# A transformer block with product-key experts on one core: picks turned into one PSUM bank, smaller one-hots, and another order at five places

## The chip, the core and the metric

The program runs on one core of a Trainium2 chip. Each time is the device time of one execution, in microseconds. The engines of a core are TensorE (PE, its weight loads PEld), VectorE (DVE), ScalarE (ACT), GpSimd (POOL) and SyncE (SP); each executes its own instructions in order and waits on semaphores for the others. PE's clock has two levels, 1.2 and 2.4 GHz; a granted clock of 1.00 in the profile is the higher, 0.50 the lower.

## What is computed

512 tokens of 1024 numbers (float32) pass through one block, cut here to what matters:

```python
h = rms_norm(x, norm1_g)
u_a, v_a, q, k, v = split(h @ w_in)          # 5 x 512 columns
a_out = spatial_gating(gelu(u_a), gelu(v_a), ...)
b_out = dilated_attention(rope(q), rope(k), v)
x = x + concat(rms_norm(a_out), rms_norm(b_out)) @ w_out
# experts: 128 x 128 keys, 8 heads, 16 picks a head
xb = rms_norm(x, norm2_g)
s = einsum('thpc,pkc->thpk', (xb @ w_query).reshape(T, 8, 2, 128), sub_keys)
s1, i1 = top_k(s[:, :, 0], 16); s2, i2 = top_k(s[:, :, 1], 16)
sc, ci = top_k((s1[..., :, None] + s2[..., None, :]).reshape(T, 8, 256), 16)
e = i1[ci // 16] * 128 + i2[ci % 16]
act = gelu(einsum('td,thkd->thk', xb, expert_u[e]))
x = x + einsum('thk,thkd->td', softmax(sc) * act, expert_v[e])
out = rms_norm(x, final_norm_g)
```

## The kernel before

float32 products are made of three: each operand is split into a high part (a cast, "hi") and a remainder (a subtraction, "lo"), and PE adds hi x hi, lo x hi and hi x lo. The stages follow one another:

- **A, to about 241 us.** `proj` (L231) makes five groups of 512 columns, each in four PSUM banks `acc`, or three and a bank of `pu`. Around its matmuls stand the eviction of q with the norm's factor (`qraw`, L270), which needs the sums of squares of all tokens (`xsq`, L309: four passes on ACT) and a root; the rotation of q and k; and the gelu of v (`va`, L373). `warm(f)` is an ACTIVATE on one element that makes ACT load the function table of f ahead of its first use; ACT holds one table at a time. Attention and the output projection follow.
- **B, to about 344 us.** `query(c)` and `scores(c)` give the key scores, `top16` sorts them on DVE.
- **C, to about 404 us.** `decode` (L648) turns the place of each pick among the candidates into its two keys. For each pick it writes row and column number 16 times beside each other (casts on ACT, L681), compares with 0..15 (L688), multiplies by the sorted list of keys (L690) and adds up in four halvings (L695, L697): 16 x 16 elements a pick and key. The dense token blocks are decoded in three calls, of 9, 9 and 6 heads times blocks; the last block's two calls of 4 lie in stage E. Meanwhile `ahead(n, limit)` issues n matmuls of the next U blocks (scores of all 384 dense tokens against 128 experts, 24 matmuls of 128 x 384 a block). For a block `part` casts uhi on ACT, ulo is made on GpSimd (`part_lo`) or later on DVE (`los`), and `flush` applies the gelu (`act`, L768). `turn(b)` (L818) then transposes the picks of 128 tokens on PE: two key numbers (idxT) and the gate gT, each through a bank of its own.
- **D, about 404 to 541 us.** The dense weights of 384 tokens and all 16384 experts, in 48 steps of 8 tokens. `hots(t8)` (L847) makes one-hots of the second key (`ohb`, 16 rows of 128) and of the first key times the gate (`oha`: 8 tokens, each with the gate's high and low part, 16 rows), both on DVE, two steps ahead. PE multiplies them in 16 matmuls (L896) into two banks, `put` evicts them on ACT (L876) to `wst`, and every fourth step is stored to DRAM in four DMAs on ACT's queue (`store`, L884). Between the steps PE makes some ten U matmuls.
- **E and F, about 546 to 1474 us.** 128 experts' rows: `vproduct` adds 18 matmuls of 128 x 512 for each to six banks `acc` (three token blocks x two halves); in E 24 U matmuls stand beside them. The last token block has its experts' rows gathered by index instead, and worked through on DVE.
- **G.** The final sum, norm and store: `final_sum`, `gain`, `root`, `finish` for each token block.

What sets the order is the code itself: the engines' instructions are issued in the order in which the loops are written, `ahead` filling in. Tiles of a pool rotate over `bufs` buffers, and an instruction that writes one waits for the readers of its last use.

Of the kernel before, what the change touches and what calls it, by code (L numbers as in the profile page):

```python
# [20 lines left out]
NB = 4  # L21
# [19 lines left out]
UVB = 4  # L41
SLOW = 0.35
# [3 lines left out]
def peer_block(ctx: ExitStack, tc: tile.TileContext, A, out):  # L46
# [182 lines left out]
    warm(AF.Copy)  # L229
# [142 lines left out]
    for b in range(NB):  # L372
        S.activation(va[:, b, :], ps[b], AF.Gelu_apprx_tanh, scale=xrs[:, b:b + 1], accum_out=lns[:, 0, b:b + 1])  # L373
# [274 lines left out]
    def decode(pool, lists, ci, outs):  # L648
# [3 lines left out]
        tl = lambda nm, dt: pool.tile(PK, dt, name=nm)  # L652

# [35 lines left out]
        for p, o in enumerate(o4):
            V.tensor_tensor(o, o, fi.rearrange("p h b s k -> p (h b) s k")[:, :, p, None, :].to_broadcast(wide),  # L690
                            op=ALU.mult)
        yield
        for w in (8, 4, 2):
            for o in o4:
                V.tensor_tensor(o[:, :, :, 0:w], o[:, :, :, 0:w], o[:, :, :, w:2 * w], op=ALU.add)  # L695
        for oh, o in zip(ohs, outs):
            V.tensor_tensor(o, oh[:, :, :, :, 0], oh[:, :, :, :, 1], op=ALU.add)  # L697
# [15 lines left out]
    HG = (3, 3, 2)  # L713
    route = [rt.tile([128, DB, H, TOPK], F32, name=f"route{i}") for i in range(3)]
# [38 lines left out]
    def pick_head(h):  # L753
# [3 lines left out]
        for n in HG:  # L757
            if h == h0 + n - 1:
                steps.append(decode(rt, dense[1][:, h0:h0 + n], ci[:, h0:h0 + n], [r[:, h0:h0 + n] for r in by_head]))
            h0 += n  # L760
# [57 lines left out]
    def turn(b):  # L818

        rows = []  # L820
        for nm, t, dt, scale in (("i2T", route[1], BF16, 1.0), ("i1T", route[0], BF16, 1.0),
                                 ("gT", route[2], F32, GSCALE)):
            ps = pr.tile([128, 512], F32, name="po" if nm == "i2T" else "tr")
            T.transpose(ps[:, :128], t[:, b].rearrange("p h k -> p (h k)"), ident)
            if nm == "i2T":

                idx = rt.tile([128, 16, 2, 8, 2], BF16, name="idxT", bufs=2)
            r = idx[:, :, len(rows), :, :] if dt is BF16 else rt.tile([128, 16, 8, 2], F32, name=nm)
            S.activation(r, ps[:, :128].rearrange("p (g t) -> p g t", t=8)[:, :, :, None].to_broadcast([128, 16, 8, 2]),
                         AF.Copy, scale=scale)  # L830
# [16 lines left out]
    def hots(t8):  # L847
# [3 lines left out]
        idx, gw = tsc[b]  # L851
# [6 lines left out]
        wide = [128, 2, 8, NK // 2, 2]  # L858
        V.tensor_tensor(a.rearrange("p (s t) (k two) -> p s t k two", s=2, two=2),  # L859
                        c[:, None, 8:16].rearrange("p o t (k two) -> p o t k two", two=2).to_broadcast(wide),  # L860
                        gw[:, g, :, :, None, :].to_broadcast(wide), op=ALU.mult)
        return a, c

# [3 lines left out]
    hot = [hots(0), hots(1)]  # L867
    ahead(24, AHEAD)
# [17 lines left out]
    for t8 in range(N8):  # L886
# [43 lines left out]
    h2 = gp.tile([128, 1024], F32, name="h2")  # L930

    def gather_routing():
# [13 lines left out]
        def decoded(h):  # L946
            return decode(gp, late[1][:, h:h + 4], gci[:, h:h + 4], [r[:, h:h + 4] for r in groute])
# [66 lines left out]
    def vsplit(e):  # L1014
        if e in vraws:
            hi = ex.tile([128, 1024], F32R, name="vhi")
            lo = ex.tile([128, 1024], F32R, name="vlo")
# [10 lines left out]

    def wsplit(e):
        if e in wmuls:  # L1030
            hi = ex.tile([128, DT], F32R, name="wahi")
            lo = ex.tile([128, DT], F32R, name="walo")
# [11 lines left out]
    for _ in range(3):  # L1044
# [66 lines left out]
    for e in range(NK):  # L1111
# [8 lines left out]
        if routing is not None:  # L1120
# [20 lines left out]
        if e == NK - 3:  # L1141
# [7 lines left out]
        if e == NK - 8:  # L1149
# [91 lines left out]
```

## Time and profile before

| | |
|---|---|
| median of 3 executions | 1488.34 us (1487.87 to 1490.42) |
| the profiled execution | 1490.96 us, span 1489.2 |
| granted clock, mean | 0.996 |
| PE busy | 1453.4 us |
| DVE busy | 1159.6 us |
| ACT busy | 641.3 us |
| GpSimd busy | 283.6 us |

The span goes from the first instruction to the last. A busy share is an average over all stages, so what an edit in one of them is worth is read from that stretch of the trace, not from this table. PE is the engine with the most work throughout; the question at each place is what it waits for there.

### The profile page before, as it was taken

Reading aid. Unit: us, or ns where it says so; the run is one execution under the profiler, and the core shown is the slowest. Engines: PE = TensorE matmul, PEld = TensorE weight load, DVE = VectorE, ACT = ScalarE, POOL = GpSimd, SP = SyncE. Lnnn points to the kernel's source line nnn. Section 1 sums busy time; section 2 is a strip of 40 time slices with the busy share of each in tenths; the row PEclk is TensorE's granted clock in tenths of the full one; section 3 lists DMA queues with packets and bytes.
Section 4 is the critical chain, followed back from the end, with each engine's and each line's share of the span. In section 5 each row is a group of like instructions: output and inputs, shape, how many; then the busy total and the mean of one; then the engine's idle time right before and its main releaser. Section 6 shows DMA issues by size and latency. Waiting matters only on the chain.

```text
span 1489.2 us, 21574 instructions
## 1 busy us (share of the span) xinstructions
PE 1453.4 (98%) x7945; PEld 1292.6 (87%) x7945; DVE 1159.6 (78%) x2415; ACT 641.3 (43%) x1088; POOL 283.6 (19%) x222
## 2 busy tenths in 40 slices
PE   8999999999899999999999999999999999999997
PEld 6878988888888899999999999999999999987785
DVE  4745554999899967779878787888787888877775
ACT  5455753344555544434333333333333333323334
POOL 0040002445500000012222222222222222211002
PEclk9999999999999999999999999999999999999999
DMA  6331032232366776469999999999999998988764
GB/s 217 106 99 57 22 114 104 86 91 96 110 230 256 261 291 214 135 228 378 355 351 329 315 338 321 327 334 336 347 326 333 331 328 308 348 286 299 250 212 160
DMA packets 128777, 358.52 MB, mean 241 GB/s; under 512 B 9120, under 2 KB 59808, under 8 KB 112288
## 3 DMA queue, kind: packets, MB, share of 16 engines
q1 hardware_dynamic: 103184, 197.75, 40.1%
q0 software_dynamic: 18432, 134.23, 23.6%
q10 hardware_dynamic: 7056, 25.18, 4.2%
q8 instruction: 62, 1.02, 0.3%
q14 instruction: 43, 0.35, 0.1%
HBM read 327.10 MB, written 30.02 MB: 240 GB/s over the span
## 4 chain that ended last, share of the span: by engine, by line
PE 78%; DVE 9%; DMA 5%; issue 3%; ACT 3%; POOL 1%; ACTq 0%; SPq 0%; DVEq 0%; POOLq 0%
PE pu L201 34%; PE acc L1041 30%; PE acc L252 6%; DMA vraw<-in_uv_dram 3%; DVE ohb L855 3%; DVE oha L859 2%; DVE ulo L181 1%; DMA uraw<-in_uT_dram 1%; PE tr L734 1%; PE pu L252 1%; PE tr L434 1%; POOL ulo L181 1%; PE acc L447 1%; DVE vlo L81 1%; DMA xt<-in_x_dram 1%
## 5 line engine op out<-in xcount | busy, mean ns | idle before, releaser
L201 PE MATMUL pu<-h2T,uhi 128*128 128x384 f32 (+2 forms) x2336 | 451.0, 342 | 3.2 <-ACT act L768 2.4
L201 PEld LDWEIGHTS pu<-h2T,uhi 128*128 128x128 f32 x2336 | 409.6, 189 | 19.4 <-ACT act L768 3.1
L987 POOL DMA_INDIRECT uv<-in_uv_dram,ei x128 | 170.6, 1333 | 830.1 <-DVE xlast L1002 318.0
L81 DVE TENSOR_TENSOR vlo<-vraw,vhi 128x1024 fp32r<-128x1024 f32 x128 | 156.8, 1225 | 154.9 <-ACT vhi L80 154.7
L80 ACT CAST vhi<-vraw 128x1024 fp32r<-128x1024 f32 x128 | 134.6, 1051 | 296.3 <-issue 188.6
L1041 PE MATMUL acc<-vhi,wahi 128*128 128x512 f32 x768 | 238.7, 391 | 1.9 <-ACT wahi L80 1.9
L1041 PE MATMUL acc<-vlo,wahi 128*128 128x512 f32 x768 | 238.2, 391 | 0.5
L1041 PE MATMUL acc<-vhi,walo 128*128 128x512 f32 x768 | 237.8, 391 | 0.0
L201 PE MATMUL pu<-h2T,ulo 128*128 128x384 f32 (+2 forms) x1168 | 234.1, 340 | 2.3 <-POOL ulo L181 2.3
L201 PEld LDWEIGHTS pu<-h2T,ulo 128*128 128x128 f32 x1168 | 203.7, 188 | 7.4 <-POOL ulo L181 2.9
L170 ACT CAST uhi<-uraw 128x1024 fp32r<-128x1024 f32 x144 | 150.7, 1047 | 61.1 <-DMA uraw<-in_uT_dram 47.6
L1041 PEld LDWEIGHTS acc<-vlo,wahi 128*128 128x128 f32 x768 | 143.8, 188 | 33.7 <-DVE vlo L81 2.4
L1041 PEld LDWEIGHTS acc<-vhi,walo 128*128 128x128 f32 x768 | 143.7, 188 | 31.5 <-DVE walo L81 0.9
L1002 DVE SCALAR_TENSOR_TENSOR xlast<-uv,dot,xlast 128x1024 f32<-128x1024 f32 x128 | 164.5, 1285 | 4.5
L1041 PEld LDWEIGHTS acc<-vhi,wahi 128*128 128x128 f32 x768 | 142.6, 188 | 26.9 <-ACT wahi L80 3.1
L768 ACT ACTIVATE act<-pu 128x384 f32<-128x384 f32 x128 | 62.9, 492 | 234.9 <-PE pu L201 234.5
L993 DVE SCALAR_TENSOR_TENSOR uv<-uv,h 128x1024 f32<-128x1024 f32 x128 | 153.7, 1219 | 6.7 <-DMA uv<-in_uv_dram,ei 6.7
L181 DVE TENSOR_TENSOR ulo<-uraw,uhi 128x1024 fp32r<-128x1024 f32 x116 | 141.5, 1220 | 22.1 <-ACT uhi L170 21.9
L181 POOL TENSOR_TENSOR ulo<-uraw,uhi 128x512 fp32r<-128x512 f32 x56 | 81.5, 1479 | 209.4 <-ACT uhi L170 203.7
L81 DVE TENSOR_TENSOR walo<-wa,wahi 128x384 fp32r<-128x384 f32 x128 | 70.7, 553 | 0.6 <-ACT wahi L80 0.6
L80 ACT CAST wahi<-wa 128x384 fp32r<-128x384 f32 x128 | 65.2, 509 | 13.0 <-DVE wa L1026 12.9
L1026 DVE TENSOR_TENSOR wa<-act,wt 128x384 f32<-128x384 f32 x128 | 70.5, 551 | 0.0
(258 smaller groups left out, 1475.4 us busy)
## 6 DMA issues: line engine op xcount, KB each, us to landing
uraw<-in_uT_dram SPq DMA_DIRECT2D x128, 512.0 KB, 5.9
vraw<-in_uv_dram SPq DMA_DIRECT2D x128, 512.0 KB, 5.3
wd<-wst ACTq DMA_DIRECT2D x48, 512.0 KB, 3.1
wt<-wd SPq DMA_DIRECT2D x32, 768.0 KB, 10.6
wraw<-in_w_in_dram SPq DMA_DIRECT2D x19, 512.0 KB, 3.6
uraw<-in_w_q_dram SPq DMA_DIRECT2D x16, 512.0 KB, 3.8
xT<-in_xT_dram SPq DMA_DIRECT2D x8, 256.0 KB, 3.9
xt<-in_x_dram SPq DMA_DIRECT2D x1, 2048.0 KB, 11.5
```

Of the source, the lines that this page charges most:

```text
L80: S.copy(hi, src)
L81: sub.tensor_tensor(lo, src, hi.bitcast(F32), op=ALU.subtract)
L170: S.copy(hi, raws[i])
L181: eng.tensor_tensor(lo[:, k, :], raws[i][:, k, :], hi[:, k, :].bitcast(F32), op=ALU.subtract)
L201: T.matmul(o, l[:, k, :], r[:, k, t0:n], start=(p == 0 and k == 0), stop=(p == 2 and k == KT - 1))
L252: T.matmul(out[b], l[:, b * 128:(b + 1) * 128], r[:, kk, :], start=(k == 0 and i == 0), stop=(k == KT - 1 and i == 2))
L768: S.activation(acts[e], o[:, :DT], AF.Gelu_apprx_tanh)
L987: G.indirect_dma_start(out=uvs[r].rearrange("p s d -> p (s d)"), out_offset=None, in_=A["uv"], in_offset=bass.IndirectOffsetOnAxis(ap=ei[: ...
L993: V.scalar_tensor_tensor(uv[:, 0, :], uv[:, 0, :], 1.0, h2, op0=ALU.mult, op1=ALU.mult, accum_out=d[:, 0:1])
L1002: V.scalar_tensor_tensor(xlast, uv[:, 1, :], d[:, 1:2], xlast, op0=ALU.mult, op1=ALU.add)
L1026: eng.tensor_tensor(wa.rearrange("p (c t) -> p c t", c=NWC), acts.pop(e).rearrange("p (c t) -> p c t", c=NWC), wts[e // WG][:, :, e % WG, ...
L1041: T.matmul(acc[b][n], l[:, c], r[:, n * 512:(n + 1) * 512], start=(e == 0 and i == 0), stop=(e == NK - 1 and i == 2))
```

## The change

1. The first `warm` loads the table of Sqrt (before: Copy's); the sums of squares of token blocks 1 and 3 are DVE's.
2. The table of Gelu is loaded before the last piece of the turning of k, and `va` is made in the order 1, 2, 3, 0 of the token blocks.
3. `decode` compares 24 rows of 8 (16 rows with 0..7 and the upper half of the list's 8 columns with 8..15) for each pick, and folds the upper half into the lower by one addition; the table `iota_v` of numbers is built on GpSimd.
4. `turn(b)` puts its three transposes side by side into one bank, tr and po by turns.
5. `oha` is ordered by token; DVE multiplies 14 of its 16 rows, and `gated()` makes the last token's two on ACT, with a column `gs` of the gate as the scale, ahead of the store.
6. Before the last four stores one more U block is worked off, and one less behind them.
7. Splits of experts 126 and 127 take buffers of the gathered rows; the last block's products of the last four experts (LASTV) come at the end, one half of the columns after the other; the norms of the other blocks are written between these; the gathered rows end one expert sooner; the last scale is made half on DVE, half on ACT, with two DMA queues.

```diff
-    warm(AF.Copy)
+    warm(AF.Sqrt)
...
-        sumsq(sq, xt[:, b, :], xss[:, b:b + 1])
+        if b % 2:
+            V.scalar_tensor_tensor(sq, xt[:, b, :], 1.0, xt[:, b, :], op0=ALU.mult, op1=ALU.mult,
+                                   accum_out=xss[:, b:b + 1])
+        else:
+            sumsq(sq, xt[:, b, :], xss[:, b:b + 1])
...
-    for _ in range(4):
+    for p in range(4):
+        if p == 3:
+            warm(AF.Gelu_apprx_tanh)
         next(turning)
         drain(gen, 2)
-    warm(AF.Gelu_apprx_tanh)
...
-    for b in range(NB):
+    for b in (1, 2, 3, 0):
         S.activation(va[:, b, :], ps[b], AF.Gelu_apprx_tanh, scale=xrs[:, b:b + 1], accum_out=lns[:, 0, b:b + 1])
...
+            oh = pool.tile([128, n, TOPK + K8, K8], BF16, name="oh", bufs=3 if pool is rt else 2)
+            flat = r.rearrange("p h b k -> p (h b) k")[:, :, :, None]
+            S.copy(oh[:, :, 0:TOPK, :], flat.to_broadcast([128, n, TOPK, K8]))
+            S.copy(oh[:, :, TOPK:, :], flat[:, :, K8:, :].to_broadcast([128, n, K8, K8]))
...
+            V.tensor_tensor(o, o, iota_v[:, None, :, :].to_broadcast([128, n, TOPK + K8, K8]), op=ALU.is_equal)
...
+            V.tensor_tensor(o[:, :, TOPK:, :], o[:, :, TOPK:, :], f[:, :, :, K8:].to_broadcast([128, n, K8, K8]),
+                            op=ALU.mult)
+            V.tensor_tensor(o[:, :, 0:TOPK, :], o[:, :, 0:TOPK, :], f[:, :, :, 0:K8].to_broadcast([128, n, TOPK, K8]),
                             op=ALU.mult)
         yield
-        for w in (8, 4, 2):
+        for o in o4:
+            V.tensor_tensor(o[:, :, K8:TOPK, :], o[:, :, K8:TOPK, :], o[:, :, TOPK:, :], op=ALU.add)
+        for w in (4, 2):
...
+        ps = pr.tile([128, 512], F32, name=("tr", "po")[b % 2])
+        for j, t in enumerate((route[1], route[0], route[2])):
+            T.transpose(ps[:, j * 128:(j + 1) * 128], t[:, b].rearrange("p h k -> p (h k)"), ident)
...
+        gs = rt.tile([128, 16, 2], F32, name="gs", bufs=2)
+        V.tensor_copy(gs[:, :, 0], gw[:, :, 7, 0, 0])
+        V.tensor_tensor(gs[:, :, 1], gT[:, :, 7, 0], gs[:, :, 0], op=ALU.subtract)
...
+        wide = [128, 7, 2, NK // 2, 2]
+        V.tensor_tensor(a[:, 0:14].rearrange("p (t s) (k two) -> p t s k two", s=2, two=2),
+                        c[:, 8:15, None].rearrange("p t o (k two) -> p t o k two", two=2).to_broadcast(wide),
+                        gw[:, g, 0:7, :, None, :].to_broadcast(wide), op=ALU.mult)
+        rest.append((a, c, gs, g))
...
+    def gated():
+        for a, c, gs, g in rest:
+            for s in range(2):
+                S.activation(a[:, 14 + s, :], c[:, 15, :], AF.Copy, scale=gs[:, g, s:s + 1])
+        rest.clear()
...
     hot = [hots(0), hots(1)]
+    gated()
     ahead(24, AHEAD)
...
         put()
         flush()
+        gated()
...
+    ahead(10 ** 6, AHEAD)
+    ahead(24, AHEAD + 5)
+    los()
     for j in range(per):
         store(j)
-    ahead(10 ** 6, AHEAD)
+    flush()
...
-    for _ in range(3):
+    for _ in range(2):
         ahead(24, AHEAD + 5)
...
+    lasts = range(NK - LASTV, NK)
+    for e in lasts:
+        vproduct(e, 2, (0,))
     for b in (0, 1):
...
+    for e in lasts:
+        vproduct(e, 2, (1,))
...
+    V.tensor_scalar(xback[2][:, :512], outs[2][:, :512], rs, None, op0=ALU.mult)
+    S.activation(xback[2][:, 512:], outs[2][:, 512:], AF.Copy, scale=rs)
```

The order of instructions on ACT at the first dense steps, before (`wst<-acc` is the eviction of a step's two banks, `act` the gelu of a U block, `uhi` the cast for a later one):

```order
L829 ACTIVATE gT<-tr 128x256
L170 CAST uhi<-uraw 128x1024
L768 ACTIVATE act<-pu 128x384
L876 ACTIVATE wst<-acc 128x128x4 x2
L170 CAST uhi<-uraw 128x1024
L876 ACTIVATE wst<-acc 128x128x4 x2
L768 ACTIVATE act<-pu 128x384
L876 ACTIVATE wst<-acc 128x128x4 x2
```

And of the change, at the same place:

```order
L849 ACTIVATE gT<-tr 128x256
L891 ACTIVATE oha<-ohb,gs 128x128 x4
L171 CAST uhi<-uraw 128x1024
L789 ACTIVATE act<-pu 128x384
L907 ACTIVATE wst<-acc 128x128x4 x2
L891 ACTIVATE oha<-ohb,gs 128x128 x2
L171 CAST uhi<-uraw 128x1024
L907 ACTIVATE wst<-acc 128x128x4 x2
```

Behind the gate's eviction gT stand four gated ACTIVATEs, two for each of the first two steps, ahead of the uhi cast; then each step's pair stands behind its evictions, or behind the gelu where there is one.

DVE at the same place, before (`gw` is the gate in two parts, `ohb` and `oha` the one-hots of a step):

```order
L836 CAST gw<-gT 128x16x16
L837 TENSOR_TENSOR gw<-gT,gw 128x16x16
L855 TENSOR_TENSOR ohb<-iota_b,idxT 128x2048
L859 TENSOR_TENSOR oha<-ohb,gw 128x2048
L855 TENSOR_TENSOR ohb<-iota_b,idxT 128x2048
L859 TENSOR_TENSOR oha<-ohb,gw 128x2048
L181 TENSOR_TENSOR ulo<-uraw,uhi 128x1024
```

And of the change:

```order
L853 CAST gw<-gT 128x128x2
L854 TENSOR_TENSOR gw<-gT,gw 128x128x2
L857 CAST gs<-gw 128x16
L858 TENSOR_TENSOR gs<-gT,gs 128x16
L876 TENSOR_TENSOR ohb<-iota_b,idxT 128x2048
L880 TENSOR_TENSOR oha<-ohb,gw 128x1792
L876 TENSOR_TENSOR ohb<-iota_b,idxT 128x2048
L880 TENSOR_TENSOR oha<-ohb,gw 128x1792
L182 TENSOR_TENSOR ulo<-uraw,uhi 128x1024
```

Two small instructions for gs are new behind gw, each oha has 1792 elements instead of 2048, and the order of the rest is the same.

ACT at the end of the dense weights, before:

```order
L876 ACTIVATE wst<-acc 128x128x4 x2
L884 DMA wd<-wst 128x1024 x4
L170 CAST uhi<-uraw 128x1024
L768 ACTIVATE act<-pu 128x384
L170 CAST uhi<-uraw 128x1024
```

And of the change:

```order
L907 ACTIVATE wst<-acc 128x128x4 x2
L171 CAST uhi<-uraw 128x1024
L915 DMA wd<-wst 128x1024 x4
L789 ACTIVATE act<-pu 128x384
L171 CAST uhi<-uraw 128x1024
```

The uhi cast has moved ahead of the four last stores.

## Rows read from the trace of the kernel before

**Rows 1.** The page's first part: busy time, share of the span and instructions of each engine.

```profile
PE 1453.4 (98%) x7945; PEld 1292.6 (87%) x7945; DVE 1159.6 (78%) x2415; ACT 641.3 (43%) x1088; POOL 283.6 (19%) x222
```

**Rows 2.** Busy time by stretches: each engine, PE's granted clock, DMA share, GB/s.

```profile
360.00:380.00 20.00, 17.72 (x90) 17.08 (x91) 19.97 (x89) 6.84 (x10) 16.54 (x8) 0.91 0.24 82
...
450.00:500.00 50.00, 48.06 (x450) 44.15 (x449) 49.39 (x45) 29.66 (x52) 0.00 (x0) 1.00 0.69 258
```

**Rows 3.** Waits of PE, 0 to 241 us: total, times, longest.

```profile
PE acc L252 <- ACT qraw L270: 2.1, 1, 2.1
PE acc L252 <- ACT va L373: 1.3, 1, 1.3
```

**Rows 4.** Waits of PE, 340 to 404 us.

```profile
PE pu L201 <- ACT act L768: 2.4, 1, 2.4
PE pu L201 <- POOL ulo L181: 2.3, 2, 2.0
PE po L824 <- DVE route L697: 1.5, 1, 1.5
PE tr L824 <- ACT idxT L829: 0.8, 1, 0.8
```

**Rows 5.** Timeline of ACT, 23 to 34 us: start, duration, idle before and releaser.

```profile
28.43 1.05 ACT L151 ACTIVATE xs<-xt 128x1024 f32<-128x1024 f32 x1
...
29.59 1.28 ACT L146 ACT_TABLE_LOAD   x1
30.88 0.30 ACT L146 ACTIVATE xrs<-xss,eps 128x4 f32<-128x4 f32 x1
```

**Rows 6.** Timeline of DVE, 364 to 404 us.

```profile
365.06 2.63 DVE L688 TENSOR_TENSOR oh<-oh,iota_b 128x2304 bf16<-128x2304 bf16 x2
...
370.13 2.92 DVE L695 TENSOR_TENSOR oh<-oh 128x1152 bf16<-128x1152 bf16 x6
...
386.85 0.96 DVE L688 TENSOR_TENSOR oh<-oh,iota_b 128x1536 bf16<-128x1536 bf16 x1 [1.42 <-ACT oh L681]
...
391.94 5.32 DVE L695 TENSOR_TENSOR oh<-oh 128x768 bf16<-128x768 bf16 x6
```

**Rows 7.** Timeline of ACT, 352 to 404 us.

```profile
354.43 2.11 ACT L681 CAST oh<-rw 128x2304 bf16<-128x2304 int32 x1 [1.84 <-DVE rw L671]
```

**Rows 8.** Groups of instructions, 404 to 540 us: busy, mean ns; idle before.

```profile
L859 DVE TENSOR_TENSOR oha<-ohb,gw 128x2048 f16<-128x2048 bf16 x47 | 57.6, 1225 | 1.6
L855 DVE TENSOR_TENSOR ohb<-iota_b,idxT 128x2048 bf16<-128x2048 bf16 x47 | 57.2, 1218 | 0.0
...
L876 ACT ACTIVATE wst<-acc 128x512 f32<-128x512 f32 x94 | 51.1, 597 | 34.8 <-PE acc L896 34.6
...
L829 ACT ACTIVATE idxT<-po 128x256 bf16<-128x256 f32 x2 | 0.8, 384 | 6.4 <-PE po L824 6.4
...
L836 DVE CAST gw<-gT 128x256 f16<-128x256 f32 x2 | 0.6, 285 | 0.0
```

**Rows 9.** Timeline of PE, steps of the dense weights (48 in all).

```profile
403.70 1.05 PE L896 MATMUL acc<-oha,ohb 128*128 128x128 f16 x16
...
406.41 1.07 PE L896 MATMUL acc<-oha,ohb 128*128 128x128 f16 x16
...
540.29 1.07 PE L896 MATMUL acc<-oha,ohb 128*128 128x128 f16 x16 [0.68 <-DVE oha L859]
```

**Rows 10.** Waits of PE, 404 to 560 us.

```profile
PE pu L201 <- ACT uhi L170: 0.5, 1, 0.5
```

**Rows 11.** Timeline of all engines, 1478 to 1485 us.

```profile
1477.98 0.39 PE L1041 MATMUL acc<-vlo,wahi 128*128 128x512 f32 x1
...
1478.21 0.39 PE L1041 MATMUL acc<-vhi,walo 128*128 128x512 f32 x1
...
1481.92 0.75 DVE L1081 TENSOR_TENSOR fin<-acc,fin 128x256 f32<-128x256 f32 x2
...
1484.70 0.49 DVE L1108 TENSOR_SCALAR fin<-fin,sd 128x512 f32<-128x512 f32 x1
```

More of the change, by code (lines that the diff above doesn't have):

```diff
@@ L41 @@
 UVB = 4
+LASTV = 4
 SLOW = 0.35
@@ L646, in candidates, with lookup_rows, decode @@
         return cand
-    def decode(pool, lists, ci, outs):
+    def lookup_rows(pool):
+        rows = pool.tile([128, 24, 8], BF16, name="iota_v")
+        for r0, r1, c0 in ((0, 16, 0), (16, 24, 8)):
+            G.tensor_copy(rows[:, r0:r1, :], iota[:, None, c0:c0 + 8].to_broadcast([128, r1 - r0, 8]))
+        return rows
+    def decode(pool, iota_v, lists, ci, outs):
         _, nh, nb, _ = PK = list(ci.shape)
@@ L758, in pick_head @@
             if h == h0 + n - 1:
-                steps.append(decode(rt, dense[1][:, h0:h0 + n], ci[:, h0:h0 + n], [r[:, h0:h0 + n] for r in by_head]))
+                steps.append(decode(rt, iota_v, dense[1][:, h0:h0 + n], ci[:, h0:h0 + n], [r[:, h0:h0 + n] for r in by_head]))
             h0 += n
@@ L857, in hots @@
                         pairs(idx[:, g]), op=ALU.is_equal)
[L858 to L861, printed above, removed]
-        return a, c
+        wide = [128, 7, 2, NK // 2, 2]
[3 more added lines that the diff above has]
+        rest.append((a, c, gs, g))
+        return a, c
+    rest = []
+    def gated():
[3 more added lines that the diff above has]
+        rest.clear()
     N8 = DT // 8
@@ L930, in peer_block @@
     h2 = gp.tile([128, 1024], F32, name="h2")
+    iota_g = lookup_rows(gp)
     def gather_routing():
@@ L946, in decoded @@
         def decoded(h):
-            return decode(gp, late[1][:, h:h + 4], gci[:, h:h + 4], [r[:, h:h + 4] for r in groute])
+            return decode(gp, iota_g, late[1][:, h:h + 4], gci[:, h:h + 4], [r[:, h:h + 4] for r in groute])
         for h in range(SOON, H):
@@ L1027, in wmul @@
                             acts.pop(e).rearrange("p (c t) -> p c t", c=NWC), wts[e // WG][:, :, e % WG, :], op=ALU.mult)
+    wlast = []
     def wsplit(e):
         if e in wmuls:
-            hi = ex.tile([128, DT], F32R, name="wahi")
-            lo = ex.tile([128, DT], F32R, name="walo")
+            if e < NK - 2:
+                hi = ex.tile([128, DT], F32R, name="wahi")
+                lo = ex.tile([128, DT], F32R, name="walo")
+            else:
+                if not wlast:
+                    wlast.append(ex.tile([128, 4, 512], F32R, name="wl", tag="uv", bufs=UVB))
+                hi, lo = (wlast[0][:, 2 * (e - NK + 2) + i, :DT] for i in range(2))
             split(hi, lo, wmuls.pop(e), V)
@@ L1164, in peer_block @@
             grs = root(gb, 2)
-        if e < NK - 2:
-            for b in range(DB):
+        if e < NK - 1:
+            for b in range(DB if e < NK - LASTV else DB - 1):
                 vproduct(e, b)
```

95 lines of the change are left out of this document (45 added, 50 removed).

## Prediction

> **What bounds the kernel now.** I read the page's engine line first, then the busy time by stretches, then PE's waits stage by stage, and at each wait the timeline of the engine that ended it. PE is busy 1453.4 us of the span [rows 1], so at most some 36 us lie outside its matmuls, and an edit on another engine pays only where PE waits for that engine or ends before the last output. Stage A (to 241 us): PE waits 2.1 us for qraw on ACT and 1.3 us for the first va [rows 3]; nothing else that the change touches. Stage C (decoding, 344 to 404): DVE is busy 19.97 us of 20 while PE has 17.72 [rows 2], and PE's four waits sum to 7.0 us [rows 4]; the granted clock over that stretch is 0.91 [rows 2], so for part of it PE ran at the lower of its two levels, 1.2 GHz. Stage D (dense weights, 404 to 540): DVE 49.39 of 50, PE 48.06, ACT 29.66 [rows 2], so DVE sets the step. In E (experts) PE is full, and what the stages before it save passes through it as a shift.
>
> **The change part by part.** *Start.* ACT makes four xsq passes, then loads the table of Sqrt (1.28 us), and takes the root at 30.88 [rows 5]; qraw is evicted behind it, and PE waits 2.1 for that. Afterwards two of the passes (1.05 each) are DVE's and the table is loaded while ACT still waits for its first input. ACT could so be ready some 3.4 us earlier (2 x 1.05 + 1.28), more than PE waits; the eviction of the first bank still stands ahead of PE, half a microsecond or less, so PE resumes about 1.8 earlier, of its 2.1. *Gelu.* The table load leaves the path and the three acc banks are freed ahead of pu, which PE needs later: its 1.3 wait goes, at most the whole of it. For A together 3.1 (bounds 2.5 and 3.4). The cover is ACT's idle time ahead of both loads; without it the gain would be 1.3 less at each. The load is priced by its row: 1.28 us, with the next ACTIVATE straight behind it [rows 5]. The Trainium skill, "ScalarE: Activation LUTs", "Rules for kernel authors", has one budget 2.7 us for each switch of table set; by that ACT would win more at either place. PE's waits cap the gain, so the sum stays; the trace shows half of that price.
>
> *Decoding.* The one-hots of the picks shrink from 16 x 16 to 24 x 8 for each pick. DVE prices: 1536 bf16 elements took 0.96 us [rows 6], 2048 took 1.218 [rows 8], that is 0.508 ns an element and 0.18 fixed, of which some 0.08 overlaps the neighbour. For nine picks (n = 9) the comparison goes from 2304 to 1728 elements, twice: 2 x 0.29 saved. The product is cut in two (1152 + 576): 2 x (0.29 - 0.10) saved. The first addition falls from 1152 to 576, the others stay: 2 x 0.29. That is 1.54; for n = 6 the same working gives 0.97; three dense decodes (9, 9, 6) 4.05. Where GpSimd's ulo runs beside them, DVE is slower: the additions of 768 elements took 5.32 against 2.92 for the larger ones of 1152 [rows 6], so shorter work there may save up to 2.5 times as much, some 6.4 in all. I take 4.9, nearer the clean price, because only the mult of the first decode and the last additions are stretched. The casts to the one-hots on ACT go from 2 x 2.11 [rows 7] to 2 x (1152 + 576 elements), some 3.5 by the slope 0.83 of [rows 8] (below), and ACT no longer waits 1.84 for rw, since DVE comes earlier: together about the 2.4 that PE waits there, and with it the half clock goes. For n = 6, DVE's wait of 1.42 for oh falls by about 0.25. The end of C, though, is set by DVE: what PE wins at its waits for act and ulo (2.4 + 2.3, [rows 4]) and in clock it would only wait longer for route (1.5 now) if DVE didn't come earlier, so DVE's saving is what counts. Two iota casts on GpSimd come long before, and cost nothing here.
>
> *Turning.* Three transposes go to one bank, one ACT wait, and no return of PE to ACT for a bank: PE's 0.8 [rows 4] goes, and ACT's gT comes about 0.55 earlier. Two DVE operations on 32 elements for gs are new; the nearest row is the gw cast of 256 at 0.285 [rows 8]; between nothing and that I take 0.15 each, 0.3, thrice in the kernel. C in sum: 4.9 + 0.25 + 0.55 - 0.3 = 5.4 (bounds 3.0 and 7.5).
>
> *Dense steps.* The 48 steps go from 403.70 to 540.29 [rows 9]: 136.59 / 47 = 2.906 each. DVE's gated one-hot loses 256 of 2048 elements: 256 x 0.508 = 0.13 a step. Those rows become two ACTIVATEs of 128 x 128 with a column as scale. Rows for ACT: 256 elements 0.384, 512 elements 0.597 [rows 8], slope 0.83 ns, so 0.28 each, 0.55 a step; ACT was busy 29.66 / 50 x 2.906 = 1.72 a step, and has 2.28 after, inside a step of 2.79 (2.906 - 0.13 + 0.013 for the two later gs). PE's own step without a wait is 406.41 - 403.70 = 2.71 [rows 9]; DVE stays the bound. Gain 47 x 0.117 = 5.5. From it goes the first step: ACT's uhi cast now stands behind four gated ACTIVATEs, which wait for the second step's one-hots, and DVE's next operation is the ulo of that cast; I put 0.7 to 1.6 of DVE idle on it, once, and take 1.2. D: 4.3 (bounds 0.5, when ACT's order eats it, below, and 6.3). What hides the ACTIVATEs is that PE needs those two rows last, 0.8 us into the step's 16 matmuls. The Trainium skill, "ScalarE: Activation LUTs", "Rules for kernel authors", speaks against this part: multiplications belong on VectorE, which is several times faster. By the rows it is right on the operation (0.55 against 0.13); but VectorE is the engine waited for, so the row on who is busy decides, unless ACT becomes the bound (third rival).
>
> *Last stores.* Four stores stand ahead of a uhi cast on ACT's queue, and PE waited 0.5 for that cast [rows 10]. Now one block's work goes first: 0.5 gained (bounds 0.3 and 0.5). The stores are issued one cast later; their data is first read several us behind them, so nothing waits for it.
>
> *Tail.* PE's last matmul starts at 1478.21; DVE reaches the last sums at 1481.92, because the roots of the other token blocks and the first half's work stand ahead of them, and scales last at 1484.70 [rows 11]. Now the last block's products of four experts come last, 24 matmuls, one in each 0.23 us (1477.98 to 1478.21), 5.4 us, and the other blocks are finished under them; by the durations of these operations DVE gets to the last sums at about PE's end + 2.2 instead of + 3.3; one of the two final scales moves to ACT. Against that, expert 127's split is needed 2.7 us earlier by PE: a wait of 0 to 0.5. I take 0.7 (bounds 0 and 1.2).
>
> **Sum.** 3.1 + 5.4 + 4.3 + 0.5 + 0.7 = 14.0, against the profiled execution's 1490.96 us (span 1489.2 and 1.8 around it): 1477.0. The median shown is 2.6 lower, so 1474.3 there. All low bounds together: 2.5 + 3.0 + 0.5 + 0.3 + 0 = 6.3, 1482.0; all high: 3.4 + 7.5 + 6.3 + 0.5 + 1.2 = 18.9, 1469.4.
>
> **Rivals.** First: ACT executes in order, and the gated pair waits for one-hots two steps ahead; behind it stand the put of the next step, the uhi cast and the gelu. With DVE only just ahead of PE, a uhi cast, the pair and the put come to some 3.0 us behind the one-hots, at a step of 2.79, so a bank may come late in each step that has a cast. For it: 20 of the 48 steps have one. Against: a PE that is late gives the pair its time back, so the loss shouldn't repeat. If it does, D gains 0 to 1: 14.0 - 3.8 = 10.2, 1478.1. Second: C's saving is taken by GpSimd. Its ulo stretches beside DVE's bf16 work; earlier DVE work moves it, doesn't end it, and PE waits for ulo (2.3, [rows 4]). Then C gives 2: 1477.7. Third, the other side: ACT becomes D's bound. It breaks even when a gated pair holds ACT 2.906 - 1.72 = 1.19 us, just twice the 0.597 of a 512-element eviction; the rest of the change (9.7) is lost too at 1.39. At 1.6 a pair the step is 3.32, D costs 47 x 0.41 = 19.5, and the time is 1488.3 + 19.5 - 9.7 = 1498. Against it: the operation has a quarter of that eviction's elements; for it: its waits, which no row shows. Fourth: the savings ahead of E are given back there, if the loads of U and V and not PE set its pace; only the tail's 0.7 would stay, 1487.6. Against it: PE's busy share there is full.
>
> **How the numbers follow.** The forecast 0.62, first rival 0.17, second 0.10, third 0.06, fourth 0.05. About 0.2% (3 us) is what a measurement of this kernel can tell. The first three cases are faster by more: 0.89; the fourth is the same: 0.05; the third slower: 0.06. The range of the forecast's bounds, 1469.4 to 1482.0, also holds the first two rivals; I widen the low end slightly, to 1468, for C's unknown contention.
>
> **What would show it.** PE's waits for qraw and the first va gone or under 0.3; in C, no clock below full, and the first dense step 8 us earlier than 403.70 (A's 3.1 and C's 5.4); a dense step of 2.79 with DVE above 49 of 50 and ACT near 41 of 50; two gated ACTIVATEs of 0.28 each; no PE wait for them beyond the first step; PE's last matmul 13 us earlier and the last scale 6 us behind it. It is wrong if a dense step is 2.9 or more, if PE waits on gated rows step after step, or if C ends less than 3 us earlier than A's shift accounts for.

## The result, and the profile after

The changed kernel took 1476.16 us (median of 6 executions, 1473.55 to 1478.14) beside 1489.0 of the kernel before (6 executions): 12.8 us less, ratio 0.9912 with a 95% interval of 0.9899 to 0.9925. 14.0 less was predicted. The profiled execution after has a span of 1474.2 us against 1489.2, 15.0 less. Where they arise is read from the same points of both traces: the last but one group of score matmuls of stage B began at 343.11 and 338.43, the first dense step at 403.70 [rows 9] and 395.09, the last at 540.29 and 526.65, PE's last matmul at 1478.21 [rows 11] and about 1464.5 (the last of six that start at 1463.36, 0.227 apart). The table's rows are for this one pair of executions.

| stretch | before | after | difference | predicted |
|---|---|---|---|---|
| A and B, to these scores | 343.11 | 338.43 | -4.7 | -3.1 |
| C, to the first dense step | 60.59 | 56.66 | -3.9 | -5.4 |
| D, first to last dense step | 136.59 | 131.56 | -5.0 | -4.3 |
| experts, to PE's last matmul | 937.92 | 937.85 | -0.1 | -0.5 |
| G, to the end of the span | 10.99 | 9.7 | -1.3 | -0.7 |

*Start.* ACT's timeline in the changed kernel, 22 to 34 us (the first rows of x have landed at 23.87):

```profile
23.87 1.06 ACT L152 ACTIVATE xs<-xt 128x1024 f32<-128x1024 f32 x1 [3.06 <-DMA xt<-in_x_dram]
...
28.79 0.30 ACT L147 ACTIVATE xrs<-xss,eps 128x4 f32<-128x4 f32 x1 [1.44 <-DVE xs L313]
29.39 2.42 ACT L271 ACTIVATE qraw<-acc,xrs 128x512 f32<-128x512 f32 x4 [0.30 <-DVE xrs L148]
```

The table load is gone from the path, but ACT now waits 1.44 us for DVE's squares. Of PE's two waits of [rows 3], 0 to 241 us, one of 0.3 is left; that for va is gone:

```profile
PE acc L253 <- ACT qraw L271: 0.3, 1, 0.3
```

The 2.1 and 1.3 of [rows 3], less the 0.3 left, make 3.1; the other 1.6 were nearly all clock. In the kernel before, PE's timeline behind its wait for qraw reads:

```profile
32.22 0.50 PE L252 MATMUL acc<-wph,thi 128*128 128x512 f32 x1 [2.06 <-ACT qraw L270]
...
33.04 0.63 PE L252 MATMUL acc<-wph,thi 128*128 128x512 f32 x1
33.47 0.63 PE L252 MATMUL acc<-wph,tlo 128*128 128x512 f32 x1
...
36.90 0.40 PE L252 MATMUL pu<-wph,tlo 128*128 128x512 f32 x1
```

and the busy time of two stretches there (granted clock behind POOL's column):

```profile
32.00:34.00 2.00, 1.78 (x6) 1.44 (x7) 1.76 (x4) 2.00 (x5) 0.00 (x0) 0.75 0.00 0
34.00:36.00 2.00, 2.00 (x6) 1.57 (x5) 1.42 (x2) 0.84 (x1) 0.00 (x0) 0.50 0.00 0
```

A matmul takes 0.63 there, 0.40 before and after it: 0.50 is the lower level, 1.2 GHz. The matmuls from 32.22 to 36.90 took 4.68 us; the same ones took 3.13 after (30.13 to 33.26), at a granted clock of 1.00.

*Decoding.* DVE's timeline, 340 to 392 us, in the changed kernel (answers to [rows 6]):

```profile
342.90 0.89 DVE L670 CAST cf<-ci 128x144 f16<-128x144 uint32 x1
...
359.50 2.03 DVE L702 TENSOR_TENSOR oh<-oh,iota_v 128x1728 bf16<-128x1728 bf16 x2
...
363.51 0.82 DVE L711 TENSOR_TENSOR oh<-oh 128x576 bf16<-128x576 bf16 x2
...
379.30 0.76 DVE L702 TENSOR_TENSOR oh<-oh,iota_v 128x1152 bf16<-128x1152 bf16 x1 [1.19 <-ACT oh L698]
...
384.80 2.81 DVE L711 TENSOR_TENSOR oh<-oh 128x384 bf16<-128x384 bf16 x2
...
390.79 1.23 DVE L853 CAST gw<-gT 128x256 f16<-128x256 f32 x1 [1.67 <-ACT gT L849]
```

The comparison of nine picks fell from 2.63 to 2.03 for two, 0.60 where 0.58 was worked out. Beside GpSimd's ulo there are still 2.81 us for two additions of 384 elements, and the small cast cf took 0.89 where it took 0.20 in the kernel before; a ulo now runs beside it (341.18 to 343.70). PE waits there for other things:

```profile
PE pu L202 <- POOL ulo L182: 2.8, 2, 2.5
PE acc L927 <- DVE oha L880: 1.1, 1, 1.1
PE pu L202 <- ACT act L789: 0.7, 1, 0.7
PE tr L843 <- DVE route L717: 0.4, 1, 0.4
```

The wait for act fell from 2.4 to 0.7; that for idxT is gone. The granted clock stayed at 1.00 through this stage, in the kernel before it was 0.50 from 362 to 364 us. That is this execution's, not the kernel's. The same decoding runs in eight traces of this case, each with a wait of 2.54 to 2.57 us for ulo at about 367 us. Behind it the clock stays at 1.00 in two (the changed kernel and g_order) and falls to the lower level in six (s_old, g_lastv3, d_two, d_alt, d_pool and best). It costs nothing that shows: from the scores to the first dense step it is 56.66 and 56.98 us in the two, 56.37 to 56.93 in the six. So PE's waits and its clock don't set the end of this stage, as the prediction said; DVE does.

*Dense steps.* Groups of instructions, 395 to 528 us (busy, mean ns | idle before):

```profile
L876 DVE TENSOR_TENSOR ohb<-iota_b,idxT 128x2048 bf16<-128x2048 bf16 x47 | 57.2, 1217 | 0.0
...
L880 DVE TENSOR_TENSOR oha<-ohb,gw 128x1792 f16<-128x1792 bf16 x48 | 52.4, 1092 | 1.6
L907 ACT ACTIVATE wst<-acc 128x512 f32<-128x512 f32 x96 | 51.7, 594 | 1.1 <-DMA wd<-wst 0.7 <-issue 0.5
...
L891 ACT ACTIVATE oha<-ohb,gs 128x128 f16<-128x128 bf16 x94 | 32.7, 400 | 25.6 <-DVE ohb L876 25.6
```

oha fell from 1225 to 1092 ns, 0.133 a step as worked out. A gated ACTIVATE takes 0.40 us, two in a row 0.69. The step is 131.56 / 47 = 2.799 (2.79 predicted). DVE is still full and PE nearly (450 to 500 us):

```profile
450.00:500.00 50.00, 49.31 (x469) 46.05 (x467) 49.35 (x48) 39.65 (x90) 0.00 (x0) 1.00 0.71 265
```

*Tail.* PE's and DVE's timelines, 1450 to 1476 us:

```profile
1456.03 3.41 PE L1089 MATMUL acc<-vl,wl 128*128 128x512 f32 x12 [0.99 <-ACT wl L81]
...
1463.36 1.52 PE L1089 MATMUL acc<-vl,wl 128*128 128x512 f32 x6
...
1465.22 0.17 DVE L148 RECIPROCAL sd<-sd 128x1 f32<-128x1 f32 x1 [2.30 <-ACT sd L147]
...
1467.36 0.74 DVE L1129 TENSOR_TENSOR fin<-acc,fin 128x256 f32<-128x256 f32 x2
...
1469.79 0.49 DVE L1244 TENSOR_SCALAR fin<-fin,sd 128x512 f32<-128x512 f32 x1
```

PE waits 0.99 ahead of expert 127, and DVE idles 2.30 in the middle of the tail.

### The profile page after: what moved, and what is told of

It reads as the page before. It is cut to its first block, busy times and chain, and to the rows that moved or that the text cites. A ratio compares the mean times of both kernels' runs of the same rounds, so it can differ in the third digit from the quotient of the medians.

```text
span 1474.2 us, 21710 instructions
## 1 busy us (share of the span) xinstructions
PE 1448.3 (98%) x7945; PEld 1289.3 (87%) x7945; DVE 1152.4 (78%) x2434; ACT 657.9 (45%) x1186; POOL 280.4 (19%) x222
## 4 chain that ended last, share of the span: by engine, by line
PE 77%; DVE 11%; DMA 5%; ACT 4%; issue 2%; POOL 0%; ACTq 0%; SPq 0%; DVEq 0%
PE pu L202 32%; PE acc L1089 31%; PE acc L253 7%; DVE ohb L876 3%; DMA vraw<-in_uv_dram 3%; DVE ulo L182 1%; DVE oha L880 1%; DMA wraw<-in_w_in_dram 1%; PE pu L253 1%; PE tr L440 1%; PE acc L453 1%; DMA uraw<-in_uT_dram 1%; PE po L453 1%; ACT uhi L171 1%; PE tr L755 1%
## 5 line engine op out<-in xcount | busy, mean ns | idle before, releaser
L82 DVE TENSOR_TENSOR vlo<-vraw,vhi 128x1024 fp32r<-128x1024 f32 x126 | 154.4, 1225 | 149.4 <-ACT vhi L81 149.1
L1089 PE MATMUL acc<-vhi,wahi 128*128 128x512 f32 x756 | 235.0, 391 | 0.0
L1089 PE MATMUL acc<-vlo,wahi 128*128 128x512 f32 x756 | 234.6, 391 | 0.2
L1089 PE MATMUL acc<-vhi,walo 128*128 128x512 f32 x756 | 234.3, 391 | 0.0
```

Of the source, the lines that this page charges most:

```text
L82: sub.tensor_tensor(lo, src, hi.bitcast(F32), op=ALU.subtract)
L1089: T.matmul(acc[b][n], l[:, c], r[:, n * 512:(n + 1) * 512], start=(e == 0 and i == 0), stop=(e == NK - 1 and i == 2))
```

## Experiments

Each ratio is to the kernel before, run on the same chip, with its 95% interval. The changed kernel has 0.9912 (0.9899 to 0.9925).

| kernel | median us | ratio | interval |
|---|---|---|---|
| a_start | 1485.31 | 0.9975 | 0.9966 to 0.9984 |
| c_decode | 1484.65 | 0.9969 | 0.9959 to 0.9979 |
| d_dense | 1483.63 | 0.9970 | 0.9958 to 0.9982 |
| g_tail | 1485.78 | 0.9981 | 0.9972 to 0.9990 |
| a_table | 1487.60 | 0.9993 | 0.9982 to 1.0004 |
| s_old | 1475.68 | 0.9907 | 0.9892 to 0.9923 |
| g_lastv3 | 1474.89 | 0.9904 | 0.9884 to 0.9923 |
| d_two | 1474.27 | 0.9900 | 0.9883 to 0.9916 |
| d_alt | 1473.12 | 0.9893 | 0.9877 to 0.9910 |
| d_pool | 1492.41 | 1.0030 | 1.0021 to 1.0040 |
| g_order | 1472.89 | 0.9893 | 0.9876 to 0.9909 |
| best | 1471.04 | 0.9875 | 0.9856 to 0.9895 |

**One part at a time.** These four are the kernel before with one part of the change each, taken from the diff as it stands.

*a_start*, parts 1 and 2:

> Only the edits of stage A (table of Sqrt and two sums of squares, table of Gelu, order of va). Theory that the stages' gains add up as the changed kernel's trace shows them: PE's wait for qraw about 0.3 us, that for the first va gone, the granted clock full from 30 to 40 us, the first matmul behind va about 5 us earlier than 84.50, the first dense step 4.7 earlier than 403.70, and the time 4.7 us less (ratio 0.9969). Rival, as the prediction had it: the two waits alone, 3.1 us (ratio 0.9979), the rest of the 4.7 being the luck of one execution.

0.9975 is 3.7 us less, with an interval of 2.4 to 5.1: it holds both 3.1 and 4.7. In its trace the wait for qraw is 0.3, that for va gone, the clock 1.00 from 28 to 40 us, and the first dense step at 399.40, 4.3 earlier. That was not yet the theory's proof: in d_dense and g_tail, where stage A is as before, PE has no listed wait for qraw and one of 0.27. What differs is when x lands, and when PE has done the products ahead of the wait. ACT's timeline in g_tail:

```profile
22.09 1.06 ACT L152 ACTIVATE xs<-xt 128x1024 f32<-128x1024 f32 x1 [2.77 <-DMA xt<-in_x_dram]
...
29.22 2.43 ACT L271 ACTIVATE qraw<-acc,xrs 128x512 f32<-128x512 f32 x4 [0.30 <-DVE xrs L148]
```

From x to qraw it is 7.13 us, as in the kernel before (24.35 to 31.48) and in c_decode; in the changed kernel 5.52. But x came at 22.09 here and at 24.35 there. PE's own place counts as much: in c_decode its last product ahead of the wait starts at 29.23 and it waits, in d_dense, with x at nearly the same time (23.30 and 23.13), at 30.56 and it doesn't. The next product in c_decode, then in d_dense:

```profile
31.17 0.50 PE L252 MATMUL acc<-wph,thi 128*128 128x512 f32 x1 [1.55 <-ACT qraw L270]
31.01 0.51 PE L252 MATMUL acc<-wph,thi 128*128 128x512 f32 x1
```

So the part shortens that chain by 1.6 us, and it pays that much only in executions in which x lands late for PE; [rows 3] showed one of these, with the slow clock on top. The group of scores at which the table's first row ends lies at 339.30 to 343.11 us in the four traces with the whole old start (the kernel before has the 343.11) and at 337.81 to 339.31 in the nine with the new one. The means are 2.2 apart, where the table's pair has 4.7.

*a_table* makes the table load alone:

```diff
-    warm(AF.Copy)
+    warm(AF.Sqrt)
```

> The kernel before with the first table load of Sqrt alone (one word of the change). In six traces so far the first rows of x land between 22.1 and 24.7 us, whatever the kernel; from there to qraw it is 7.13 us in the kernel before and 5.5 with both edits of the start. Theory that the table load is most of it: 5.85 here. Rival, as the prediction counted: the two squares taken from ACT are worth 2.1, the table 1.28, so 5.85 here and 3.75 with both; with 5.5 measured for both, DVE's squares then have a wait of their own. [...]

ACT's timeline:

```profile
23.34 1.06 ACT L151 ACTIVATE xs<-xt 128x1024 f32<-128x1024 f32 x1 [2.78 <-DMA xt<-in_x_dram]
...
29.19 2.43 ACT L270 ACTIVATE qraw<-acc,xrs 128x512 f32<-128x512 f32 x4 [0.31 <-PE acc L252]
```

From x to qraw it is 5.85, to the last digit, though here qraw waited 0.31 for PE in place of 0.30 for DVE. The table is 1.28 of the 1.6; the two squares moved to DVE are worth 0.3, not 2.1: the wph cast stays between ACT's two, and the root waits for DVE's last square. The time can't be told from no change.

*c_decode*, part 3:

> Only the smaller one-hots of decode (24 x 8 in place of 16 x 16). Theory that the gains add up: DVE wins about 4.6 us in the three dense decodes, the first dense step comes 3.5 us earlier than 403.70, the time falls by 3.5 (ratio 0.9976). Rival: on its own the edit wins more, since PE's wait of 2.4 for act and the slow clock behind it go too: 5.4 us (ratio 0.9964). Second rival: GpSimd's ulo takes the gain: 2 us or less.

0.9969 is 4.6 less (3.1 to 6.1): nearer to 3.5 than to 2, and 5.4 is not excluded by the time. By the trace, from the same scores (340.99) to the first dense step (396.66) it took 55.67 us, where the kernel before took 60.59: 4.9 less. PE's wait for act is gone; it waits 2.84 for ulo instead, and the clock falls behind that wait (0.50 from 370 to 372 us), so the slow clock has moved and not gone. By the trace it wins alone more than the 3.5 I had left for it in the changed kernel, and less than 5.4. GpSimd does not eat it.

*d_dense*, parts 4 and 5:

> Only the transposes in one bank and the gated rows on ACT (order of the last stores as before). Theory that the gains add up: a dense step of 2.80 in place of 2.906, two ACTIVATEs of 0.35 to 0.40 each, the last dense step 5.0 us earlier than 540.29, the time 5.0 less (ratio 0.9966). Rival: the step's gain shows only because the stages before it were shortened; then the step stays at 2.85 or more and the gain is under 3 us.

0.9970, 4.5 less (2.7 to 6.2). The first dense step at 400.97, the last at 532.58: 131.61 / 47 = 2.800 a step, the same as in the changed kernel. The gain does not hang on the other parts. Ahead of the first dense step these parts win nothing: from the scores to that step it is 60.63, in the kernel before 60.59.

*g_tail*, part 7:

> Only the edits behind the experts: splits of the last two in other buffers, the last block's products last, norms under them, the last scale on two engines. Theory that the gains add up: PE waits about 1.0 us ahead of expert 127, its end comes 1.0 later, from PE's last matmul to the end of the span 1.3 less than before's 11.0; net 0.3 less or nothing that can be measured (ratio 0.9995 to 1.0005). Rival: the wait ahead of expert 127 comes from the shortened stages before it; then it is absent here and 1.3 us are gained (ratio 0.9991).

2.8 us less (1.5 to 4.2), more than either theory allowed. The wait ahead of expert 127 is there (0.87), so the rival's reason is wrong. From PE's last matmul (1471.37) to the end it is 9.6, 1.4 less than before's 10.99, nearly as in the changed kernel (1.3). The rest lies where neither theory had anything: between the last U matmuls and the tail. PE's waits in the kernel before, 1300 to 1490 us:

```profile
PE acc L1041 <- ACT wahi L80: 1.9, 3, 1.4
```

One of 1.3 to 1.5 stands about 90 us behind the last U block in all five kernels with the old tail (before, a_start, c_decode, d_dense, a_table), and in none with the new one. The new tail ends the gathered rows an expert sooner and changes their rate; which of these edits moves the wait was not tried apart.

Added up, the four parts alone make 15.6 us, together, with part 6, they make 12.8. Each has an interval of 1.3 to 1.8 to either side, so that is no proof that they get in each other's way.

**The stores.** *s_old* is the changed kernel without part 6:

```diff
-    ahead(10 ** 6, AHEAD)
-    ahead(24, AHEAD + 5)
-    los()
     for j in range(per):
         store(j)
-    flush()
+    ahead(10 ** 6, AHEAD)
...
-    for _ in range(2):
+    for _ in range(3):
```

> The changed kernel with the old order around the last four stores (stores first, three U blocks behind). Theory of the prediction: the order gains 0.5 us; here PE waits 0.5 us or more for uhi behind the stores, and the time is 0.5 more. Rival, from the changed kernel's trace (PE waits 1.32 us for uhi three blocks later, where the kernel before waited 0.50): the U blocks' loads are what is late behind a shorter dense stage, the order only moves the wait; here it is 0.9 to 1.3 too, and the time the same.

PE's wait for uhi behind the dense steps is 0.84 at 533.50, in the changed kernel 1.32 at 549.90, three blocks later and behind a uhi cast that waited 3.85 for its load. s_old's line, then the changed kernel's:

```profile
533.50 3.07 PE L202 MATMUL pu<-h2T,uhi 128*128 128x384 f32 x16 [0.84 <-ACT uhi L171]
549.90 3.05 PE L202 MATMUL pu<-h2T,uhi 128*128 128x384 f32 x16 [1.32 <-ACT uhi L171]
```

The times are the same (0.9907 and 0.9912). The order moves the wait to the next late load, and the 0.5 is not won.

**What a gated row costs.** *d_two* gives ACT the rows of two tokens in each step, *d_alt* in every second step:

```diff
-        wide = [128, 7, 2, NK // 2, 2]
-        V.tensor_tensor(a[:, 0:14]...
+        n = 6                      # d_alt: 7 - t8 % 2
+        wide = [128, n, 2, NK // 2, 2]
+        V.tensor_tensor(a[:, 0:2 * n]...
...
-            for s in range(2):
-                S.activation(a[:, 14 + s, :], c[:, 15, :], AF.Copy, scale=gs[:, g, s:s + 1])
+            for t in range(n, 8):
+                for s in range(2):
+                    S.activation(a[:, 2 * t + s, :], c[:, 8 + t, :], AF.Copy, scale=gs[:, g, t - 6, s:s + 1])
```

> The changed kernel with the rows of two tokens a step (four of oha's 16 rows) made on ACT, 12 left to DVE. By the changed kernel's rows DVE has 2.80 - 0.13 = 2.67 us a step, ACT 2.27 + 0.69 = 2.96. Theory that ACT's busy time is the next bound and a pair costs it what its row says (0.69 for two): a step of 2.96 to 3.0, the dense stage 7.5 to 9.5 us longer than the changed kernel's, the time near 1484 to 1486. Rival, the prediction's price of 0.28 for one and 0.55 for two: ACT has 2.6 to 2.85, the step is PE's 2.71 to 2.85, and the time is 4 us less to 2 more than the changed kernel's.

> The changed kernel with two tokens' rows on ACT in every second step, one token's in the others. DVE has 2.735 a step on average, ACT 2.61, PE 2.71. Theory that the step is the busiest engine's own time: 2.74 and 2.8 us less than the changed kernel (ratio to before some 0.002 lower). Rival, the order on ACT: with 2.61 of 2.74 busy and waits for the one-hots between, ACT doesn't get its evictions done in time, the step stays at 2.80 or grows.

d_two's step is (525.80 - 395.40) / 47 = 2.774, d_alt's (525.55 - 395.71) / 47 = 2.763; neither is longer than the changed kernel's 2.799. The theory of d_two fell: it added 0.69 for a second pair. In d_alt the rival is out; the theory's 2.74 was met to 0.02. By their times (0.9900 and 0.9893) the two can't be told from the changed kernel; what they win is read from the traces. ACT's timeline in d_two, and its busy time there:

```profile
443.27 1.30 ACT L893 ACTIVATE oha<-ohb,gs 128x128 f16<-128x128 bf16 x4
444.44 1.11 ACT L909 ACTIVATE wst<-acc 128x512 f32<-128x512 f32 x2
```

```profile
450.00:500.00 50.00, 49.86 (x480) 46.78 (x477) 47.77 (x49) 49.48 (x129) 0.00 (x0) 1.00 0.75 272
```

Four take 1.30 and hold the next operation 1.17 back: 0.29 each, as predicted for one, while a single one lasts 0.40. ACT is busy 49.48 of 50 and still keeps up. So ACT could carry twice what the change gave it, and is then as good as full. In d_alt PE is busy 50.00 of 50 from 450 to 500 us, so what is left of this stage is PE's:

```profile
450.00:500.00 50.00, 50.00 (x486) 47.13 (x484) 49.20 (x49) 45.34 (x110) 0.00 (x0) 1.00 0.74 272
```

**GpSimd beside DVE.** *d_pool* leaves ulo to GpSimd in the dense steps:

```diff
     drain(turn(0))
-    prog["pool"] = False
...
             hot.append(hots(t8 + 2))
-        los()
...
+    prog["pool"] = False
+    los()
     ahead(10 ** 6, AHEAD)
```

> The changed kernel with ulo left to GpSimd during the dense steps (20 blocks, two operations each) in place of DVE. DVE has 2.80 - 0.48 = 2.32 a step, PE 2.71. Theory that GpSimd and DVE hold each other up, as the stretched rows in the decoding suggest (operations of DVE 1.0 to 1.2 us longer where a ulo begins or ends, ulo 5 instead of 2.5): each of 40 operations costs DVE 1 us or more, the step is 2.9 to 3.3 and PE waits for ulo; the time 5 to 20 us more than the changed kernel's. Rival: the two share without loss, the step is PE's 2.71 and the time 4 us less.

1.0030 against 0.9912 is 17.6 us more than the changed kernel; the first dense step is at 395.94, the last at 545.15, and the step is 149.21 / 47 = 3.175. DVE's timeline in d_pool:

```profile
441.98 2.06 DVE L879 TENSOR_TENSOR oha<-ohb,gw 128x1792 f16<-128x1792 bf16 x1
443.95 2.29 DVE L875 TENSOR_TENSOR ohb<-iota_b,idxT 128x2048 bf16<-128x2048 bf16 x1
446.28 1.09 DVE L879 TENSOR_TENSOR oha<-ohb,gw 128x1792 f16<-128x1792 bf16 x1
```

and GpSimd's:

```profile
441.43 3.74 POOL L182 TENSOR_TENSOR ulo<-uraw,uhi 128x512 fp32r<-128x512 f32 x2 [6.05 <-ACT uhi L171]
```

Two DVE operations beside one pair of ulo operations are 0.97 and 1.07 longer, and the pair takes 3.74. The step is 0.85 above DVE's own 2.32, 40 us in all, 1.0 for each of the 40 ulo operations. A pair so costs DVE 2.0, more than the 1.22 in which DVE makes both halves itself; the rival is out.

**The tail.** *g_lastv3* sets LASTV to 3, *g_order* changes the order of the sums:

```diff
-    for b in (0, 1):
-        sums[b] = ex.tile([128, 2, 4], F32, name="ss", bufs=4)
-        sumsq(junk, xback[b], sums[b][:, 0, 0:1])
-        rs = inv_root(ex, sums[b][:, 0, 0:1], 1024)
+    total(0)
+    for b in (0, 1):
+        rs = inv_root(ex, sums[b][:, 0, 0:1], 1024)
+        if b == 0:
+            total(1)
+        else:
+            final_sum(2, 0, 0, 512)
...
-        if b == 0:
-            final_sum(2, 0, 0, 512)
```

where `total(b)` holds the two lines of the sum of squares.

> The changed kernel with the last block's products of the last three experts, not four, put at the end. Expert 127's first product then comes six matmuls (1.36 us) later. Theory that PE's wait of 0.99 ahead of it costs nothing, since DVE's queue behind the products of blocks 0 and 1 sets the end: the wait is gone, those products end 0.4 us later, and so does the span. Rival: the wait is on the path; the end comes 1.0 earlier.

> The changed kernel with the tail's sums written in another order: the squares of token block 1 on ACT ahead of the first half of block 2, whose sum comes between the scalings of blocks 0 and 1. In the changed kernel's trace DVE idles 2.30 us for block 1's root, because ACT makes block 2's squares first, and reaches the last sums 2.5 us behind PE's last matmul. Theory that DVE's queue, not PE, sets the tail: the last sums start within 0.7 us of PE's end, from PE's last matmul to the end of the span 9.7 becomes 7.7, the time 2 us less (ratio to before 0.0013 lower). Rival: the stores' way to DRAM sets the end; the span's end moves by less than 0.5.

DVE's timeline in g_order, 1452 to 1475 us (PE's last matmuls start at 1463.12, the last about 1464.26):

```profile
1462.01 0.16 DVE L148 RECIPROCAL sd<-sd 128x1 f32<-128x1 f32 x1
...
1464.68 0.76 DVE L1129 TENSOR_TENSOR fin<-acc,fin 128x256 f32<-128x256 f32 x2
...
1467.12 0.49 DVE L1249 TENSOR_SCALAR fin<-fin,sd 128x512 f32<-128x512 f32 x1
```

The idle 2.30 is gone, the last sums start 0.4 behind PE's last matmul, and the end is 7.2 behind it, 2.5 nearer: the theory of DVE's queue holds, and the stores' way is not the bound. (By time alone, 0.9893, it can't be told from the changed kernel.) In g_lastv3 PE's wait is gone too, and its last matmul came at about 1461.5; yet from the first sum of block 0 (1456.19) to the end (1472.4) it took 16.2, as in the changed kernel (1457.88 to 1474.2, 16.3). So behind these products DVE sets the end, not PE. Whether the wait itself costs anything stays open: the stretch from the last U matmuls to that first sum was 147.8 there, 149.2 in the changed kernel, 147.2 in g_tail, which has the wait, and that spread is larger than the 0.4 in question.

**Both.** *best* is the changed kernel with d_alt's and g_order's edits:

> The changed kernel with one or two tokens' rows on ACT by turns and the tail's sums in the other order. If both gains add up as measured in the traces (a step of 2.763 in place of 2.799, 1.7 us; the span 2.5 nearer to PE's end), 4 us less than the changed kernel: ratio to before 0.988 to 0.989, time near 1471. Rival: what the dense stage wins is lost again behind it, since the U blocks come late there (PE's wait for uhi): 2.5 less only.

1471.04 us, 0.9875: faster than the changed kernel: the two intervals (to 0.9895, and from 0.9899) do not meet. Its step is (525.61 - 395.75) / 47 = 2.763 and its end 7.2 behind PE's last matmul. PE's wait for uhi behind the dense steps is 1.46, 0.14 more than the changed kernel's, so a little of D's gain is given back there.

## Why the prediction was right, and where its terms were off

The time fell by 12.8 where 14.0 was forecast, and of the five rows of the table four moved clearly the forecast way; the experts' moved by 0.1. Step by step:

- **Start and Gelu, 3.1.** In this pair of traces 4.7, alone 3.7 (2.4 to 5.1). Both waits went, that for qraw not quite for the reason given. Two things were off. The step "two of the passes are DVE's" was credited 2 x 1.05; a_table and the changed kernel show 0.3 for it and 1.28 for the table. Of the 1.8 that PE's wait for qraw lost, 1.6 is then the shorter chain, and the rest comes of x and PE's own place in the two executions: that it was 1.8, as worked out, is luck. And the wait of 2.1 was taken for the kernel's, when it is one execution's: x landed between 22.1 and 24.7 us in the 14 traces of this case, and the four with the old start have waits of 2.06, 1.55, 0.27 and none. That execution also lost 1.55 us to the slow clock behind its wait, which I had seen in stage C but not looked for here.
- **Decoding and turning, 5.4.** 3.9 in the trace, 4.9 alone for the decoding. On DVE the three decodings gave 1.26, 1.78 and 1.39 (by how much earlier the operations behind each start than those ahead), that is 4.4 of the 4.9 forecast, nearer the clean price as chosen. The first of them runs in stage B (from 323.01 us in the kernel before) and not in C; the small additions cand behind it took 2.82 beside a ulo, where they took 0.58. 0.55 went back between the cast cf, which met GpSimd's ulo, and rw, turning gave 0.4 and not 0.55, and the cast of gw (1.23, where it took 0.97) and gs (0.17 and 0.18) took 0.6 where 0.3 was set. The terms left out were the collisions that earlier DVE work runs into: the second rival's mechanism, at a sixth of its price. The sign "no clock below full" was met here and not in six other traces of the same code, and the time didn't hang on it.
- **Dense steps, 4.3.** 5.0. The step was forecast at 2.79 and is 2.799; DVE's idle time for the ulo behind the four gated ACTIVATEs is 0.58, where 1.2 was set aside. The first rival, ACT's order holding PE up in each step with a cast, did not occur: PE has five waits for oha, 3.4 us, and none for the gated rows. The third rival priced ACT's limit at 1.19 a pair; d_two puts two pairs into each step at 1.17, loads ACT to 49.48 of 50 and is no slower, which fits that price.
- **Last stores, 0.5.** Nothing: the wait was moved to a later block and is 0.8 longer than before (0.5 longer than in s_old). I read the wait's releaser (a cast behind four stores) and not what was late next, the U loads.
- **Tail, 0.7.** 1.3 behind PE's end, against 0.99 of waiting ahead of expert 127, where 0 to 0.5 was forecast; and 1.9 us of waits among the last experts went, which the sum did not have. DVE reached the last sums 2.9 us behind PE's last matmul's start, 2.5 behind its end, where 2.2 was worked out.

That the total came out rests in part on errors that cancel: in this pair of traces A was 1.6 too small, C 1.5 too large. A's surplus is the luck of one execution, the slow clock above all.

## What to carry to other kernels

A wait read from one execution is a sample: before its length becomes a gain, look what released it, and if a transfer stands behind it, see in a second trace where that transfer lands. The same holds for a slow clock, and for its absence. When work leaves the engine that sets the pace, its new place is judged by how long it holds the next operation there (0.29 for four in a row), not by the duration of one alone (0.40), and by what idle time that engine has. In a tail, follow the one queue that orders the last sums: another order of a few lines gave 2.5 us there, more than the rest of the edits behind the experts won behind PE's last matmul.

## What the runs showed of the hardware

- ACT with a column as scale: 0.40 us for 128 x 128 from SBUF, 0.29 from one to the next. The Trainium skill, "ScalarE: Activation LUTs", "What ACT_TABLE_LOAD costs", has 280 ns + 0.833 ns an element for one pointer operand, and an overlap of about 93 ns back to back; an estimate from these figures is 0.387 and 0.29. The traces agree within 0.02.
- GpSimd and DVE: one ulo pair beside DVE's operations with two inputs makes two of these about 1.0 us longer. The Trainium skill, "SBUF — State Buffer", "Terms", says that the two share a pair of ports, that one holds it for its whole instruction and that the other is blocked meanwhile. 0.97 and 1.07 on DVE, each less than the 1.26 of a GpSimd operation without a neighbour (2.52 for two), fit that; no run tells it from another cause.
- PE's granted clock fell to 0.50 behind a wait of 2.06 us in stage A and behind one of 2.38 in stage C of the kernel before, but stayed at 1.00 behind one of 2.54 in the changed kernel (367.54), where it fell behind 2.56 in d_two (368.06). In c_decode it stayed at 1.00 behind 1.55 (31.17) and fell to 0.50 behind 1.50 (1405.91). The length of the wait alone does not decide it; what else does was not tried.
